# A hybrid decoder step on one core: the new tokens' state products moved from TensorE to VectorE, with the states transposed

## The chip, the cores and the metric

The kernel runs on one core of a Trainium2 chip. A core has five engines that each work through their own instructions in order and wait for one another by semaphores: PE (TensorE, matrix products; PEld is its weight load), DVE (VectorE), ACT (ScalarE), POOL (GpSimd) and SP (SyncE, which here only issues transfers). 16 DMA engines move data between the chip's memory (HBM) and the core's own memory. The metric is the device time of one execution in microseconds. All arithmetic is fp32. A large product is three passes over parts of its operands (a high part `hi` and a rest `lo` each: hi x hi, lo x hi, hi x lo).

## The reference

One layer of a decoder works on 512 prompt tokens and on 8 new tokens (a batch of 8 sequences, one token each): a feed-forward block, a token mixer, a second feed-forward block, each between norms. The mixer has two branches with 4 heads of 128 x 128 each. Every new token carries, for each branch and head, a state S of 128 (key dimension d) x 128 (value dimension e), 8 x 4 x 2 = 64 states in all. With one token per sequence the reference comes down to this for each state:

```
retention:   S' = gamma * S + k v^T                      o = q S'
DeltaNet:    S1 = exp(g) * S ;  u = beta * (v - k S1)
             S' = S1 + k u^T                             o = q S'
```

gamma is a constant of the head, exp(g) and beta belong to the token and head. o (per head normalized over e, then gated) goes on through the branch products `br`; S' is an output. The prompt tokens go through chunked forms of the same recurrences, which hold most of the mixer's small products.

## The kernel before

Features lie on partitions, tokens along the free dimension: 520 columns, 512 prompt and 8 new tokens, in two halves of 260. A product of weights with all tokens goes k-step by k-step, each step 2 halves x 3 passes of 128x260 (`passes`, L404 to L410). After each step the program calls `tick` (L223): this advances `now` by one, lets the weight prefetch go on, and resumes every spawned task (a Python generator) whose due time has come. A task that yields n is resumed n ticks later. So the order of instructions on each engine is fixed when the program is written: a task's instructions stand between two steps of the running product. `LATER` (L46) shifts single yields of single tasks by hand.

Weights come in raw tiles of 512 KB over SP (`load_to`, L270 to L289; two buffers), ACT makes the high part (L350), DVE the rest (L351); the splits run `AHEAD` = 2 products in front. Working tiles of 2 KB per partition come from one pool of 68 slots (`slot`, L247).

In the mixer (`mixer`, L1023) the projections follow `proj_order`: gates; then per head k, q, v of DeltaNet with their convolution; then per head RQ, RK, RV of retention; then RG and GZ (output gates), 4 each; then GR with the retention branch products and GG with the DeltaNet branch products. Each is 8 ticks. When a head's operands are there, its prompt part is spawned (`ret_head`, `gdn_head`); those tasks send small products to PE between the steps, and DVE, ACT and POOL work on their results. `gdn_head` needs the inverse of triangular matrices (`inverse`, L1484), whose substitution runs on POOL.

The new tokens' part has two tasks.

- `decode_gdn` (L1703) starts after the last DeltaNet projection: convolution and norms for 8 tokens, then `state_products` (L1654): states are loaded over SP, head by head, and for every token and head PE takes S as the stationary operand and the columns k and q as the moving one (L1665). From the two columns of results DVE makes u and o; o uses the identity q S' = q S1 + (q.k) u, with q.k from a column sum on PE (L1600). Then the norm, and `dec_done`.
- `decode_ret` (L1670) starts after the last RV and does the same with q alone.

After that each task runs `state_update` (L1629): u (or v) is transposed to rows, written to a scratch in HBM, read back as a broadcast to all partitions (L1635), the state is loaded a second time (L1651), ACT multiplies it with the decay (L1699 or L1757), DVE adds the outer product with d on partitions (L1643: broadcast row times the column k), and POOL issues the transfer out (L1646). A step of this is 18 ticks, eight steps for each branch.

The branch products wait at the end of each output gate stage (`while out not in done: self.tick()`) until `finish_decode` has put the new tokens' 8 columns into their operands.

Of the kernel before, what the change touches and what calls it, by code (L numbers as in the profile page):

```python
# [7 lines left out]
F32 = mybir.dt.float32  # L8
# [39 lines left out]
    ("decode_gdn", 0): {1: 8, 2: 2, 10: 3},  # L48
# [122 lines left out]
class Kernel:  # L171
# [851 lines left out]
    def mixer(self, xs, r, plus_next, x_from):  # L1023
# [26 lines left out]
        self.rdec = c.tile([P, 3, H, DEC], F32, name="rdec")  # L1050
        self.go, self.ro = [None] * H, [None] * H
# [5 lines left out]
        self.dec_done = set()  # L1057
        tiles, gate, lead = {}, {}, []

        def project(kind, h):  # L1060
# [16 lines left out]
            elif kind == RV:  # L1077
# [4 lines left out]
                if h == H - 1:  # L1082
                    self.spawn(self.decode_ret())
# [534 lines left out]
    def broadcast_rows(self, cols, name):  # L1618

        nc = self.nc  # L1620
        pt = self.bank("tr32")
        self.tr(pt[0:32, 0:P], cols)
        rows = self.slot(name, (32, P))
        nc.vector.tensor_copy(rows, pt[0:32, 0:P])
        d = self.dram.tile([32 * P], F32, name=self.name(name))
        nc.sync.dma_start(out=d.rearrange("(r e) -> r e", e=P), in_=rows)
        return d

    def state_update(self, rows, k, src, decay, out):  # L1629

        nc = self.nc
        for i in range(8):
            h, b0 = i // 2, 4 * (i % 2)
            rb = self.slot("rb", (P, 4, P))
            nc.sync.dma_start(  # L1635
                out=rb.rearrange("p b e -> p (b e)"), in_=rows[i * 512 : (i + 1) * 512].unsqueeze(0).to_broadcast([P, 512])
            )
            s = self.load_state(src, i)
            yield 14
            decay(s, h, b0)  # L1640
            yield 4
            for b in range(4):
                nc.vector.scalar_tensor_tensor(  # L1643
                    out=s[:, b, :], in0=rb[:, b, :], scalar=k[:, h, b0 + b : b0 + b + 1], in1=s[:, b, :], op0=ALU.mult, op1=ALU.add
                )
            nc.gpsimd.dma_start(out=out[:, h, b0 : b0 + 4, :], in_=s)  # L1646

    def load_state(self, src, i):
        h, b0 = i // 2, 4 * (i % 2)
        s = self.slot("sd", (P, 4, P))  # L1650
        self.nc.sync.dma_start(out=s, in_=src[:, h, b0 : b0 + 4, :])  # L1651
        return s

    def state_products(self, src, rhs, n):  # L1654

        nc = self.nc
        acc = self.cpool.tile([P, 32 * n], F32, name=self.name("sp"))
        load = lambda h: [self.load_state(src, i) for i in (2 * h, 2 * h + 1)]
        nxt = load(0)
        yield 12  # L1660
        for h in range(H):
            s, nxt = nxt, load(h + 1) if h < H - 1 else None
            ps = self.bank("sp")
            for b in range(DEC):
                nc.tensor.matmul(ps[:, b * n : (b + 1) * n], s[b // 4][:, b % 4, :], rhs(h, b), start=True, stop=True)  # L1665
            nc.vector.tensor_copy(acc[:, h * DEC * n : (h + 1) * DEC * n], ps[:, 0 : DEC * n])
            yield 14
        self.prod = acc

    def decode_ret(self):  # L1670
        nc, c = self.nc, self.cpool
        q, k, v = (self.rdec[:, i] for i in range(3))
        ks = c.tile([P, H, DEC], F32, name="rks")
        nc.vector.tensor_scalar(ks, k, DK_SCALE, None, ALU.mult)
        qk = self.const("rqk", [P, 32])
        nc.vector.tensor_tensor(qk, q, ks, ALU.mult)
        yield from self.state_products(self.a["sret"], lambda h, b: q[:, h, b : b + 1], 1)
        acc = self.prod
        t = c.tile([P, H, DEC], F32, name="rdo")
        nc.vector.tensor_tensor(t, v, self.column_sums(qk, 32), ALU.mult)  # L1680
        for h in range(H):
            nc.vector.scalar_tensor_tensor(
                out=t[:, h, :], in0=acc[:, h * 8 : h * 8 + 8], scalar=1.0 - 2.0 ** (-5.0 - h), in1=t[:, h, :], op0=ALU.mult, op1=ALU.add
            )
# [10 lines left out]
        rows = self.broadcast_rows(v.rearrange("p h b -> p (h b)"), "vrow")  # L1695
        yield 6

        def decay(s, h, b0):
            nc.scalar.mul(s, s, 1.0 - 2.0 ** (-5.0 - h))  # L1699

        yield from self.state_update(rows, ks, self.a["sret"], decay, self.a["srets"])

    def decode_gdn(self):  # L1703
# [20 lines left out]
        kq = c.tile([P, H, DEC, 2], F32, name="gkq")  # L1724
        rs4 = rs.rearrange("p (t h b) -> p t h b", t=2, b=DEC)
        kn = c.tile([P, H, DEC], F32, name="gkn")
        tt(kn, k, rs4[:, 1], ALU.mult)
        nc.vector.tensor_copy(kq[:, :, :, 0], kn)
        nc.vector.scalar_tensor_tensor(out=kq[:, :, :, 1], in0=q, scalar=DK_SCALE, in1=rs4[:, 0], op0=ALU.mult, op1=ALU.mult)
        qk = self.const("gqk", [P, H, DEC])  # L1730
        tt(qk, kn, kq[:, :, :, 1], ALU.mult)
        yield from self.state_products(self.a["sgdn"], lambda h, b: kq[:, h, b, :], 2)
        pm2 = self.prod.rearrange("p (h b t) -> p h b t", b=DEC, t=2)
        pqk = self.column_sums(qk, 32)
        eg, beta = self.dgb[:, 0], self.dgb[:, 1]
# [142 lines left out]
```

## Time and profile before

| | |
|---|---|
| runs shown | 1217.87, 1218.39 (median), 1218.42 us |
| profiled execution | span 1218.5 us; 0.1 us above the median, nothing is shown around it |
| PE / PEld busy | 1189.1 us (98%) / 1176.9 us (97%) |
| DVE / ACT / POOL busy | 899.6 us (74%) / 573.7 us (47%) / 277.1 us (23%) |
| transfers | 170.87 MB, mean 140 GB/s |
| mean granted clock of PE | 0.990 |

The page of a profile has the busy time of each engine, 40 slices of the span, the transfer queues, the chain of work that ended last (followed back from the last instruction), and the costliest groups of instructions. A row such as `L1665 PE MATMUL sp<-gkq,sd` is line 1665 of the kernel, the engine, the operation, and output<-inputs by the program's names. A row of a timeline begins with its start and its length in us. A row of windows begins with a stretch of time in us from the span's start.

### The profile page before, as it was taken

To read this page: it belongs to the slowest core of one execution; us is meant where nothing else is said; L and a number is where in the kernel's file an instruction comes from. 1 tells how busy PE (TensorE), PEld (TensorE's weight loads), DVE (VectorE), ACT (ScalarE), POOL (GpSimd) and SP (SyncE) were. 2 spreads that over 40 slices of the span, in tenths; PEclk is the share of its full clock that TensorE was granted. 3 is DMA by queue.
4 is the path that set the end of the run, shared out by engine and by line. 5 is a ranking of instruction groups with operands and counts; after the bars stand their busy time and mean duration, and the time that the engine had idled before them with its cause. 6 is when DMAs were issued, how large, how long until landed. Compare 5 with 4: busy or idle time off the path is not lost.

```text
span 1218.5 us, 25498 instructions
## 1 busy us (share of the span) xinstructions
PE 1189.1 (98%) x9937; PEld 1176.9 (97%) x9937; DVE 899.6 (74%) x1933; ACT 573.7 (47%) x1195; POOL 277.1 (23%) x502
## 2 busy tenths in 40 slices
PE   8999999999999999999999999999999999999995
PEld 7999999999999999999999999998999999999994
DVE  8988888776548787877666667546888888867554
ACT  6655666553335564313234334334565666653330
POOL 4211111000005148745541112203311111000003
PEclk8999999999999999999999999999999999999998
DMA  6787777133352533332444564342587777332352
GB/s 191 210 203 178 192 176 185 45 100 96 96 171 60 176 105 107 117 97 89 116 133 144 175 195 172 114 157 85 152 229 190 188 183 192 85 92 81 96 168 70
DMA packets 79689, 170.87 MB, mean 140 GB/s; under 512 B 17104, under 2 KB 20016, under 8 KB 79568
## 3 DMA queue, kind: packets, MB, share of 16 engines
q1 hardware_dynamic: 67280, 144.95, 37.4%
q0 software_dynamic: 12288, 24.29, 11.7%
q8 instruction: 78, 1.28, 0.4%
q14 instruction: 43, 0.35, 0.1%
HBM read 157.37 MB, written 11.83 MB: 139 GB/s over the span
## 4 chain that ended last, share of the span: by engine, by line
PE 88%; DVE 6%; ACT 2%; issue 1%; DMA 1%; POOL 1%; SPq 0%; DVEq 0%; ACTq 0%; POOLq 0%
PE sv L408 10%; PE sv L409 10%; PE sv L410 10%; PE p L408 7%; PE p L410 7%; PE p L409 7%; PE dn L408 7%; PE dn L409 7%; PE dn L410 7%; DVE wlo L351 2%; PE br L408 1%; PE br L409 1%; PE br L410 1%; PE g L409 1%; PE g L410 1%
## 5 line engine op out<-in xcount | busy, mean ns | idle before, releaser
L408 PE MATMUL p<-xhl,whi 128*128 128x260 f32 x784 | 231.0, 295 | 0.0
L409 PE MATMUL p<-xhl,whi 128*128 128x260 f32 x784 | 222.0, 283 | 1.4 <-DVE xhl L506 1.4
L410 PE MATMUL p<-xhl,wlo 128*128 128x260 f32 x784 | 221.3, 282 | 1.7 <-DVE wlo L351 1.7
L351 DVE TENSOR_TENSOR wlo<-raw,whi 128x1024 fp32r<-128x1024 f32 (+2 forms) x121 | 142.3, 1182 | 37.7 <-ACT whi L350 35.9
L408 PE MATMUL sv<-th,w 128*128 128x260 f32 x592 | 167.2, 282 | 0.5 <-ACT q L833 0.5
L409 PE MATMUL sv<-tl,w 128*128 128x260 f32 x592 | 167.1, 282 | 0.0
L410 PE MATMUL sv<-th,w 128*128 128x260 f32 x592 | 167.0, 282 | 0.0
L409 PEld LDWEIGHTS p<-xhl,whi 128*128 128x128 f32 x784 | 148.4, 189 | 2.0 <-DVE xhl L506 1.8
L410 PEld LDWEIGHTS p<-xhl,wlo 128*128 128x128 f32 x784 | 147.9, 189 | 2.1 <-DVE wlo L351 2.1
L408 PEld LDWEIGHTS p<-xhl,whi 128*128 128x128 f32 x784 | 148.1, 189 | 0.7
L350 ACT CAST whi<-raw 128x1024 fp32r<-128x1024 f32 (+2 forms) x121 | 116.4, 971 | 31.3 <-DMA raw<-dn_in 16.9
L369 DVE TENSOR_TENSOR w<-s,w 128x512 fp32r<-128x512 f32 x148 | 101.5, 688 | 37.9 <-ACT w L368 36.5
L307 POOL DMA_DIRECT2D s<-gu_in x74 | 65.1, 973 | 282.4 <-DMA s<-gu_in 143.8
L410 PE MATMUL dn<-hh,wlo 128*128 128x260 f32 x448 | 126.6, 283 | 1.2 <-DVE wlo L351 1.2
L408 PE MATMUL dn<-hh,whi 128*128 128x260 f32 x448 | 127.0, 283 | 0.0
L409 PE MATMUL dn<-hl,whi 128*128 128x260 f32 x448 | 126.7, 283 | 0.0
L409 PE MATMUL sv<-xhl,w 128*128 128x260 f32 x444 | 125.5, 283 | 0.0
L408 PE MATMUL sv<-xhl,w 128*128 128x260 f32 x444 | 125.4, 282 | 0.0
L410 PE MATMUL sv<-xhl,w 128*128 128x260 f32 x444 | 125.0, 281 | 0.0
L408 PEld LDWEIGHTS sv<-th,w 128*128 128x128 f32 x592 | 111.4, 188 | 0.9 <-ACT q L833 0.7
L410 PEld LDWEIGHTS sv<-th,w 128*128 128x128 f32 x592 | 111.6, 188 | 0.0
L409 PEld LDWEIGHTS sv<-tl,w 128*128 128x128 f32 x592 | 111.2, 188 | 0.0
(408 smaller groups left out, 3230.4 us busy)
## 6 DMA issues: line engine op xcount, KB each, us to landing
raw<-gu_in SPq DMA_DIRECT2D x50, 512.0 KB, 5.0
raw<-win_in SPq DMA_DIRECT2D x49, 512.0 KB, 3.6
s<-gu_in SPq DMA_DIRECT2D x74, 256.0 KB, 5.7
s<-gu_in POOLq DMA_DIRECT2D x74, 256.0 KB, 5.4
raw<-dn_in SPq DMA_DIRECT2D x32, 448.0 KB, 3.4
a<-gu_in SPq DMA_DIRECT2D x37, 256.0 KB, 5.9
x<-x SPq DMA_DIRECT2D x32, 260.0 KB, 5.1
raw<-dn_in SPq DMA_DIRECT2D x16, 512.0 KB, 3.7
```

The costliest lines, as they stand in the source:

```text
L307: self.nc.gpsimd.dma_start(out=out, in_=term, accum_op=ALU.add)
L350: self.nc.scalar.copy(hi[:, ks], t[:, ks])
L351: self.nc.vector.tensor_tensor(lo[:, ks], t[:, ks], hi[:, ks].bitcast(F32), ALU.subtract)
L369: nc.vector.tensor_tensor(w[:, 1], t[i], w[:, 0].bitcast(F32), ALU.subtract)
L408: mm(ps, hi[:, k, :], xh, start=first, stop=False, skip_group_check=more)
L409: mm(ps, hi[:, k, :], xl, start=False, stop=False, skip_group_check=more)
L410: mm(ps, lo[:, k, :], xh, start=False, stop=last, skip_group_check=more)
```

## The change

The states are laid out with the value dimension e on partitions (the host's transposition, done for inputs and outputs, is not part of the time). Then k S and q S are sums along the free dimension.

- `state_products`, `state_update`, `load_state` and `broadcast_rows` go, and with them L1665, both q.k column sums and the second load of each state.
- `row_scratch` transposes k and q columns on PE, copies them on DVE and writes them to a scratch in HBM over SP: once for DeltaNet (64 rows), once per head for retention (16 rows).
- `state_tile` loads four states of a head (256 KB) and the two broadcast tiles of rows of the same size.
- `state_dot` is a multiplication over 128x512 and a reduction over the last 128, both on DVE. `state_add` is the outer product's addition: four DVE instructions with the row k and the column v or u, and then the transfer out over POOL.
- Retention runs one task per head, spawned at its RV; a task waits until the one before is done. Each head has two halves of four tokens: load, 9 ticks, decay on ACT, 2 ticks, addition, 1 tick, dot with q (L1643's work and the output are now in the same pass).
- DeltaNet runs eight steps: load, 12 ticks, decay on ACT, 3 ticks, dot with k and u, 1 tick, addition, 1 tick, dot with q.
- `LATER` loses the entry 10 of `decode_gdn`.

The core of the diff:

```diff
-    ("decode_gdn", 0): {1: 8, 2: 2, 10: 3},
+    ("decode_gdn", 0): {1: 8, 2: 2},
...
-                if h == H - 1:
-                    self.spawn(self.decode_ret())
+                self.spawn(self.decode_ret(h))
...
+    def row_scratch(self, cols, n, name):
+        nc = self.nc
+        rows = self.slot(name, (n, P))
+        pt = self.bank("tr64")
+        self.tr(pt[0:n, 0:P], cols)
+        nc.vector.tensor_copy(rows, pt[0:n, 0:P])
+        d = self.dram.tile([n * P], F32, name=self.name(name))
+        nc.sync.dma_start(out=d.rearrange("(r e) -> r e", e=P), in_=rows)
+        return d
+    def state_tile(self, src, h, b0, rows):
+        nc = self.nc
+        s = self.slot("sd", (P, 4, P))
+        nc.sync.dma_start(out=s, in_=src[:, h, b0 : b0 + 4, :])
+        out = [s]
+        for r0 in rows[1:]:
+            t = self.slot("rb", (P, 4, P))
+            nc.sync.dma_start(
+                out=t.rearrange("p b e -> p (b e)"), in_=rows[0][r0 * P : (r0 + 4) * P].unsqueeze(0).to_broadcast([P, 4 * P])
             )
+            out.append(t)
+        return out
+    def state_dot(self, out, s, rows, to):
+        nc = self.nc
+        nc.vector.tensor_tensor(to, s, rows, ALU.mult)
+        nc.vector.tensor_reduce(out=out, in_=to, axis=AX.X, op=ALU.add)
+    def state_add(self, s, krow, col, out):
+        for b in range(4):
+            self.nc.vector.scalar_tensor_tensor(
+                out=s[:, b, :], in0=krow[:, b, :], scalar=col[:, b : b + 1], in1=s[:, b, :], op0=ALU.mult, op1=ALU.add
+            )
+        self.nc.gpsimd.dma_start(out=out, in_=s)
...
+        while len(self.ret_rows) < h:
+            yield 0
+        yield 2
+        both = self.small("rqk", [P, 2, DEC])
+        nc.vector.tensor_copy(both[:, 0], self.rdec[:, 0, h, :])
+        nc.vector.tensor_scalar(both[:, 1], self.rdec[:, 1, h, :], DK_SCALE, None, ALU.mult)
+        rows = self.row_scratch(both.rearrange("p t b -> p (t b)"), 2 * DEC, "rrow")
+        yield 6
+        v = self.rdec[:, 2, h, :]
+        for b0 in (0, 4):
+            s, qb, kb = self.state_tile(self.a["sret"], h, b0, (rows, b0, DEC + b0))
+            yield 9
+            nc.scalar.mul(s, s, 1.0 - 2.0 ** (-5.0 - h))
+            yield 2
+            self.state_add(s, kb, v[:, b0 : b0 + 4], self.a["srets"][:, h, b0 : b0 + 4, :])
+            yield 1
+            self.state_dot(self.rdo[:, h, b0 : b0 + 4], s, qb, qb)
+        self.ret_rows.append(h)
...
+        tt(kq[:, 0], k, rs4[:, 1], ALU.mult)
+        nc.vector.scalar_tensor_tensor(out=kq[:, 1], in0=q, scalar=DK_SCALE, in1=rs4[:, 0], op0=ALU.mult, op1=ALU.mult)
+        rows = self.row_scratch(kq.rearrange("p t h b -> p (t h b)"), 64, "grow")
+        yield 6
...
+        for i in range(8):
+            h, b0 = i // 2, 4 * (i % 2)
+            bs = slice(b0, b0 + 4)
+            s, kb, qb = self.state_tile(self.a["sgdn"], h, b0, (rows, h * DEC + b0, 32 + h * DEC + b0))
+            yield 12
+            for b in range(4):
+                nc.scalar.activation(s[:, b, :], s[:, b, :], AF.Copy, scale=eg[:, h, b0 + b : b0 + b + 1])
+            yield 3
+            self.state_dot(u[:, h, bs], s, kb, self.slot("sk", (P, 4, P)))
+            tt(u[:, h, bs], v[:, h, bs], u[:, h, bs], ALU.subtract)
+            tt(u[:, h, bs], u[:, h, bs], beta[:, h, bs], ALU.mult)
+            yield 1
+            self.state_add(s, kb, u[:, h, bs], self.a["sgdns"][:, h, bs, :])
+            yield 1
+            self.state_dot(o[:, h, bs], s, qb, qb)
```

More of the change, by code (lines that the diff above doesn't have):

```diff
@@ L1646, in state_update @@
[L1646 to L1654, printed above, removed]
-        nc = self.nc
[L1657 to L1668, printed above, removed]
@@ L1694, in decode_ret @@
         self.dec_done.add(RG)
[L1695 to L1701, printed above, removed]
     def decode_gdn(self):
@@ L1751, in decode_gdn @@
         self.dec_done.add(GZ)
-        rows = self.broadcast_rows(u.rearrange("p h b -> p (h b)"), "urow")
-        yield 6
-        def decay(s, h, b0):
-            for b in range(4):
-                nc.scalar.activation(s[:, b, :], s[:, b, :], AF.Copy, scale=eg[:, h, b0 + b : b0 + b + 1])
-        yield from self.state_update(rows, kn, self.a["sgdn"], decay, self.a["sgdns"])
     def finish_decode(self, kind):
```

67 lines of the change are left out of this document (12 added, 55 removed).

## The prediction

> **What bounds the kernel now.** I read the page first (busy shares, then the chain that ended last), then the windows around the new tokens' work, then single lines.
>
> ```profile
> span 1218.5 us, 25498 instructions
> PE 1189.1 (98%) x9937; PEld 1176.9 (97%) x9937; DVE 899.6 (74%) x1933; ACT 573.7 (47%) x1195; POOL 277.1 (23%) x502
> PE 88%; DVE 6%; ACT 2%; issue 1%; DMA 1%; POOL 1%; SPq 0%; DVEq 0%; ACTq 0%; POOLq 0%
> ```
>
> TensorE carries 88% of the chain, so an instruction taken from PE shortens the program by its own length, as long as nothing else then arrives late. VectorE is only 74% busy overall, but that is a mean over stages. The stage of this change runs from about 488 to 772 us. The windows give, after each stretch and its length, the busy time of PE, PEld, DVE, ACT and POOL:
>
> ```profile
> 430.00:490.00 60.00, 60.00 (x508) 60.00 (x507) 48.83 (x131) 32.02 (x87) 38.93 (x84) 1.00 0.34 100
> 505.00:530.00 25.00, 25.00 (x229) 24.55 (x228) 21.27 (x62) 6.75 (x10) 14.74 (x38) 1.00 0.34 111
> 530.00:567.00 37.00, 36.67 (x339) 36.07 (x337) 25.10 (x78) 9.08 (x20) 17.35 (x49) 1.00 0.32 95
> 567.00:629.00 62.00, 62.00 (x555) 60.69 (x555) 42.15 (x124) 21.24 (x43) 28.60 (x80) 1.00 0.38 116
> 629.00:663.00 34.00, 34.00 (x294) 33.35 (x294) 22.33 (x72) 13.58 (x34) 11.25 (x30) 1.00 0.46 141
> 663.00:772.00 109.00, 109.00 (x930) 108.46 (x929) 72.40 (x179) 41.87 (x84) 15.96 (x25) 1.00 0.54 172
> ```
>
> At 81% DVE (48.83 of 60) PE still runs without a gap. Where DVE needs more, it becomes the chain: in 396 to 413 us, the convolution stage, the chain is
>
> ```profile
> by line: DVE cv L1276 36.0%; POOL rs L465 13.3%; ACT cv L1274 12.9%; issue 10.5%; PE rb L477 9.3%; DVE cin L1268 7.6%; DVE wlo L351 7.2%; DVE rows L1167 3.9%; DVE rb L557 2.5%; PE p L410 2.3%; PE p L408 0.7%; PE p L409 0.7%; DVEq L1184 0.1%
> ```
>
> So the question is how much room DVE has in the stage that the change fills.
>
> **What is removed.** The state products (L1665), 64 products in two passes each, eight groups of 16 passes on PE:
>
> ```profile
> L1665 PE MATMUL sp<-gkq,sd x64: 165/251/251, 515.5 to 567.0; 128*128 128x2 f32 x64
> L1665 PE MATMUL sp<-rdec,sd x64: 166/250/271, 582.6 to 632.9; 128*128 128x1 f32 x64
> 515.63 1.68 PE sp L1665 x16
> L1600 PE MATMUL cs<-gqk,ones x2: 190/232/273, 586.5 to 586.5; 128*128 128x32 f32 x2
> 511.66 0.44 PE tr L1162 x4
> ```
>
> A group holds the chain for 1.68 us: 8 x 1.68 = 13.4 us. The two column sums of the q.k products (232 ns a pass, overlapped) and two row transposes go, five row transposes come (0.44 / 4 = 0.11 each): about nothing. PE's side is -13.4 us. Groups lie at 515, then three before 567, three before 629, one at 631.
>
> **What is added on DVE.** Twenty-four dots (8 for retention, 16 for DeltaNet), each a multiplication and a reduction over 128x512. The trace has the multiplication's form but no reduction:
>
> ```profile
> 514.69 0.67 DVE L1434 TENSOR_TENSOR gkd<-gkd,cols 128x512 f32<-128x512 f32 x1
> 515.29 0.68 DVE L1437 TENSOR_TENSOR cv<-tr,cols 128x512 f32<-128x512 f32 x1
> L1353 DVE BATCH_NORM_STATS2 bs<-po 128x6 f32<-128x128 f32 x16 | 4.4, 274 | 6.2 <-ACT ro L1350 6.2
> L1643 DVE SCALAR_TENSOR_TENSOR sd<-rb,gkn,sd x32: 332/343/348, 630.2 to 738.5; 128x128 f32<-128x128 f32 x32
> 630.21 1.12 DVE L1643 SCALAR_TENSOR_TENSOR sd<-rb,gkn,sd 128x128 f32<-128x128 f32 x4
> 770.57 1.14 DVE L1643 SCALAR_TENSOR_TENSOR sd<-rb,rks,sd 128x128 f32<-128x128 f32 x4
> 504.44 0.18 DVE L1728 COPY gkq<-gkn 128x32 f32<-128x32 f32 x1
> ```
>
> Back to back a 512-wide pass takes 0.60 (514.69 to 515.29). For the reduction the nearest rows bound it by four statistics passes over 128 elements (4 x 0.274 = 1.10) above, and below by half a two-input pass (0.30), since it has one input instead of two. I take 0.65, the pass that also streams 512 elements once: a dot is 1.25 us, ends 0.9 and 1.7. Together 30 us. The page "VectorE: DVE Perf Modes" of the Trainium skill (perf-mode tier table) lists the reduction at one element a cycle only, the rate it lists for a two-input pass in this type; no run here shows that yet.
>
> The 16 state additions (1.13 us each, 18 us) are not new but move: L1643 ran at 630 to 772, behind everything; now each stands in front of its dot. ACT's decays move with them, on an engine 25 to 40% busy in these windows.
>
> **Where it lands.** A tick is one step of the running product. In the old order the DeltaNet products start at the tick 53 before the last value projection (RV, head 3), and the retention output is due 78 ticks after it:
>
> ```profile
> L1651 SPq DMA_DIRECT2D sd<-sgdn_in x16: 327/424/433, 502.6 to 719.6; - x16
> L1080 POOL COPY rdec<-rv x4: 189/981/1120, 487.2 to 566.3; 128x8 f32<-128x8 f32 x4
> 652.43 0.19 DVE L1615 COPY rdr<-cb 128x32 f32<-128x32 f32 x1 [1.63 <-PE cb L1614]
> ```
>
> That is 1.2 us a tick before 566 and 1.1 after. Retention: 2 + 6 + 2 x (9 + 2 + 1) = 32 ticks a head, one head after the other, from 488 to 57 ticks behind 566, about 629. A head is two dots, two additions and three small operations: 2.5 + 2.26 + 0.5 = 5.3 us; four in 141 us are 0.15 us per us. Its output then is ready at tick 67, twelve ticks earlier than before, so the wait for it ahead of the branch products goes. DeltaNet: eight steps of 17 ticks, from about 528 to 665: 2 x 1.25 + 1.13 + 2 x 0.18 = 4.0 us a step, 0.235 us per us. Its output comes at tick 99, needed at about 176: no wait. With what the old order had there taken out (copies, the u chain, three additions after 629):
>
> - 505 to 530: DVE 21.3 + 3.8 - 0.2 = 24.9; PE 25 - 1.7 = 23.3
> - 530 to 567: DVE 25.1 + 0.385 x 37 - 0.5 = 38.8; PE 37 - 5.0 = 32.0
> - 567 to 629: DVE 42.2 + 23.9 - 2 = 64.1; PE 62 - 5.0 = 57.0
> - 629 to 663: DVE 22.3 + 8.0 - 4.4 = 25.9; PE 34 - 1.7 = 32.3
>
> In the first three, 124 us long, DVE needs 127.8: it sets the pace, +3.8 in place of PE's -11.7. The fourth is PE's, -1.7. DVE can end the third late and catch up in the fourth (6.4 us of room) by as much as it may lag without stopping PE. The old trace shows such a lag:
>
> ```profile
> 498.44 0.29 PEld L1614 LDWEIGHTS cb<-cst,gdm 64*128 64x128 f32 x2
> 499.72 0.47 PEld L1539 LDWEIGHTS pV<-pack,AT 32*32 32x32 f32 x16
> 503.32 0.21 DVE L1615 COPY gdr<-cb 128x64 f32<-128x64 f32 x1
> 504.53 0.18 DVE L1729 SCALAR_TENSOR_TENSOR gkq<-dcv,gdr 128x32 f32<-128x32 f32 x1
> ```
>
> The norm's columns leave PE at 498.7 and DVE takes them at 503.3: 4.6 us behind. That lends -4.5.
>
> After 663 DVE, ACT and the queues lose the old updates, but PE is full there (108.5 of 109): nothing to gain.
>
> **New waits.** row_scratch multiplies on DVE and transposes on PE in one tick, with no step between. PE stands there until DVE has come through its backlog, and all products behind it in PE's order wait. For DeltaNet the rows above price it: PE reaches the place at about 499.7, kq is done at 504.7, so up to 5.0 us. Afterwards DVE has about 2 us of work in hand and PE's next results come 5 us later, so about 3 us of DVE time is lost. Retention has four such places; their lag is not in the trace. Between 0 and 5 each, I take 1.4, as two ticks (2.3 us) have passed since the previous dot. Together 3 + 5.6 = 8.6, bounds 0 and 24. No row prices them better.
>
> The queues:
>
> ```profile
> L1635 SPq DMA_DIRECT2D rb<-urow x8: 327/420/432, 609.8 to 719.1; - x8
> DMA to landing us min/median/max: 3.9/5.0/6.7
> SPq L287 <- DVE wlo L351: 96.4, 16, 10.5
> L1646 POOL DMA_DIRECT2D sgdns_out<-sd x8: 539/542/626, 631.6 to 739.2; - x8
> L1360 POOL TENSOR_TENSOR rsr<-var,mhalf 128x4 f32<-128x4 f32 x4 | 4.2, 1045 | 3.9 <-DVE gs L1480 2.6 <-DVE rks L1674 1.3
> ```
>
> SP: each step now issues a state and two broadcasts, 9 or 12 ticks (10 or 13 us) ahead of use, where it was 14; landing takes 5 to 7 us, but SP stands in front of weight loads, up to 10.5 us.
>
> I price this at nothing: the total of such transfers stays 48 of 256 KB (16 states instead of 32, 32 broadcasts instead of 16), and the landing hides under the ticks. POOL's output transfers stand behind DVE's additions, ahead of the powers and the inverse's steps; POOL is 47% busy there (28.60 of 62), so nothing too.
>
> **Sum.** +3.8 - 1.7 - 4.5 + 8.6 = +6.2 us on the profiled 1218.5, which lies 0.1 above the median 1218.39 of the runs, so 1224.6; I say **1225**. The dot's ends move it by about 20 x 0.35 = 7 down and 20 x 0.45 = 9 up, as some 20 dots lie in the three windows.
>
> **Rivals.**
> - *DVE takes it all in its gaps* (faster): PE keeps its -13.4 less three short stops of 1.4, 1209 (1203 to 1216). It decides once DVE's need in the three windows, 127.8, falls to PE's 112.3 plus the lag it can owe, 4.5: 11 us less, a dot of 0.7, or the cheap dot (-7) with a debt of 8.5. For it: 81% ran without a gap, and the weight splits (L351) are made two products ahead, so a debt there may last longer than the 4.6 us seen. Against: three windows over 100%, and the stop at DeltaNet's rows.
> - *Even*: the lag and a cheap reduction eat just the overload, 1218 (1216 to 1221).
> - *Late transfers*: an SP that stands up to 10.5 us in front of a weight load lets states and rows land after 10 us; ACT and DVE stand in order behind them:
>
> ```profile
> ACT sd L1699 <- DMA sd<-sret_in: 3.7, 2, 2.1
> ```
>
>   Two of the eight old decays waited, 1.85 each, under a lead of 14 ticks. If all eight do under 9, 15 more: 1240. Against: six did not.
> - *The clock*: after a stop PE runs slower for a while:
>
> ```profile
> 411.00:413.60 2.60, 1.20 (x10) 1.15 (x10) 2.44 (x10) 0.20 (x1) 0.17 (x1) 1.00 0.01 2
> 422.00:424.00 2.00, 2.00 (x13) 1.98 (x13) 1.93 (x4) 2.00 (x11) 0.00 (x0) 0.63 1.02 384
> 424.00:426.00 2.00, 2.00 (x11) 2.00 (x11) 1.97 (x5) 1.53 (x9) 1.74 (x2) 0.51 0.54 204
> ```
>
>   PE stood 1.4 us, and nine us later the clock was 0.63 and 0.51 for 2 us each, 0.74 + 0.98 = 1.7 us lost. Three such dips after the new stops give 1230. The Trainium skill's page "TensorE: Matmul & The Clock Gate" (Part 1) has the gate halve the clock after an idle window of about 3.4 us; by that only the stop of 5 us would count. The trace has a dip after a shorter stop.
>
> **Chances.** Forecast (1221 to 1232) 0.40, all in gaps 0.28, even 0.20, late transfers 0.08, clock 0.04. A measurement here tells about 0.2% (2.4 us) from no change. So faster 0.28, the same 0.20, slower 0.52. The range reaches into both signs: 1206 to 1242.
>
> **What would show it.** Right: 505 to 629 with DVE above 95% busy, PE waiting for DVE at the row transposes (5 us at DeltaNet's), the chain there on DVE lines, and 13.4 us of L1665 gone. The reduction's row settles its price. Wrong: DVE under 90% with PE's waits still there (then the stops are the cost), waits of ACT or DVE for states and rows (the transfers), or PE full through the stage and a time near 1207.

## The result, and the profile after

| | before | after |
|---|---|---|
| median of the runs | 1218.41 us | 1265.22 us (1263.48 to 1265.87) |
| ratio | | 1.0383, 95% interval 1.0371 to 1.0396 |
| profiled execution, span | 1218.5 us | 1264.1 us |
| mean granted clock of PE | 0.990 | 0.972 |

The change makes the kernel 46.8 us slower. The profile's first part and the chain of the kernel after:

```profile
span 1264.1 us, 25318 instructions
PE 1194.7 (95%) x9808; PEld 1180.7 (93%) x9808; DVE 934.6 (74%) x1985; ACT 573.8 (45%) x1195; POOL 282.4 (22%) x502
PE 69%; DVE 16%; issue 5%; ACT 5%; DMA 2%; POOL 2%; SPq 1%; DVEq 0%; ACTq 0%; POOLq 0%
```

PE has 129 instructions less and yet 5.6 us more of busy time, and its share of the chain falls from 88% to 69%. The stretches that the prediction used, in the kernel after (busy PE, PEld, DVE, ACT, POOL, then PE's granted clock):

```profile
505.00:530.00 25.00, 22.48 (x183) 21.71 (x183) 19.07 (x63) 7.76 (x14) 10.43 (x28) 0.87 0.42 131
530.00:567.00 37.00, 29.80 (x242) 29.44 (x243) 31.27 (x85) 8.70 (x20) 19.19 (x42) 0.90 0.51 148
567.00:629.00 62.00, 48.61 (x376) 47.18 (x376) 46.12 (x134) 17.21 (x37) 26.69 (x66) 0.86 0.42 137
629.00:663.00 34.00, 25.60 (x206) 24.56 (x206) 27.05 (x69) 11.78 (x28) 14.71 (x43) 0.80 0.45 145
```

No engine is full: in the first three stretches DVE is busy 96.5 of 124 us (78%), PE 100.9 (81%), and PE's clock lies at 0.86 to 0.90. That is the prediction's own sign for "the stops are the cost". What PE waits for from 470 to 800 us, first in the kernel before, then in the kernel after (total us, times, longest):

```profile
PE pV L1560 <- DVE pack L1552: 0.3, 1, 0.3
```

```profile
PE tr L1163 <- DVE rqk L1665: 20.8, 4, 7.7
PE pS L1458 <- DVE AT L1455: 4.6, 2, 4.0
PE cs L1601 <- DVE rdo L1648: 4.2, 1, 4.2
PE pV L1540 <- DVE pack L1530: 3.6, 2, 2.7
PE tr L1163 <- DVE gkq L1716: 2.5, 1, 2.5
```

The five row transposes (L1163) hold PE for 23.3 us, the head chains and the column sums for most of another 18. The longest single stop, on PE and on DVE:

```profile
573.12 0.38 PE L1454 MATMUL pu<-cv,TT 128*128 128x128 f32 x2
581.16 0.38 PE L1163 MATMUL tr<-cst,rqk 128*16 128x128 f32 x1 [7.66 <-DVE rqk L1665]
```

```profile
568.57 2.02 DVE L1653 SCALAR_TENSOR_TENSOR sd<-rb,rdec,sd 128x128 f32<-128x128 f32 x4
571.48 0.43 DVE L1293 TENSOR_TENSOR rp<-p,cos 128x260 f32<-128x260 f32 x1 [0.89 <-DMA sgdns_out<-sd]
...
574.85 1.22 DVE L351 TENSOR_TENSOR wlo<-raw,whi 128x1024 fp32r<-128x1024 f32 x1
575.99 0.68 DVE L1647 TENSOR_TENSOR rb<-sd,rb 128x512 f32<-128x512 f32 x1
576.71 0.69 DVE L1648 TENSOR_REDUCE rdo<-rb 128x4 f32<-128x512 f32 x1
...
580.87 0.16 DVE L1664 COPY rqk<-rdec 128x8 f32<-128x8 f32 x1
580.94 0.17 DVE L1665 TENSOR_SCALAR rqk<-rdec 128x8 f32<-128x8 f32 x1
```

PE is through with its work at 573.5 and asks for `rqk`, two instructions of 0.16 us. They stand in DVE's order behind the rotary products, a weight split, a dot and the pieces of two head chains: 9.4 us without a gap. Ahead of that the addition took 2.02 us instead of the 1.1 of others, and a slot that an output transfer still held cost 0.89. PE pays for the whole line, not for the instruction that it needs. Right behind the stop, in stretches of 2 us, come PE's slow ones (the clock had fallen while PE still stood, first row):

```profile
576.00:578.00 2.00, 0.00 (x0) 0.00 (x0) 1.90 (x6) 0.00 (x0) 1.69 (x6) 0.61 0.35 66
582.00:584.00 2.00, 2.00 (x11) 2.00 (x11) 0.00 (x0) 0.00 (x0) 0.00 (x0) 0.50 0.02 4
588.00:590.00 2.00, 2.00 (x11) 2.00 (x10) 0.00 (x0) 0.15 (x1) 0.00 (x0) 0.50 0.04 8
590.00:592.00 2.00, 2.00 (x18) 2.00 (x18) 1.40 (x7) 0.44 (x1) 0.00 (x0) 0.97 0.02 4
```

For 9 us after the restart PE gets half its clock (11 passes in 2 us instead of 18), and DVE, which had work for 9 us without a gap, has almost none until 590. This stop thus is paid twice, and the engine that caused it then starves.

**An account.** For each profile I divide 470 to 800 us into slices of 10 us and add up what PE stood ("stood") and, as time lost to the clock, (1 - granted clock) x busy PE of each slice ("clock"). Both, less the 0.3 of the kernel before, less the products that are gone (13.4, or 6.7 where one part of the change is made) should be the difference of the spans from 1218.5. It is, within 3.4 us, for every kernel run. The last five columns are of the one profiled execution, the first two of all runs; the profiled one can lie off the median (idle dots 4.5 us above it, halves together 5.2 below). A run's time is 1.7 to 1.85 us longer than its span (after: 1265.87 and 1264.1), so the profiled execution before, of which only the span is on record, lies by this some 1.8 us above its median, not 0.1, and the last column is lower than the medians would give by about as much:

| kernel | median us | ratio (95%) | stood | clock | products | sum | span - 1218.5 |
|---|---|---|---|---|---|---|---|
| after | 1265.22 | 1.0371 to 1.0396 | 41.6 | 21.1 | -13.4 | +49.0 | +45.6 |
| before, five stops | 1241.65 | 1.0178 to 1.0209 | 14.4 | 5.5 | 0 | +19.6 | +21.0 |
| before, 24 idle dots | 1223.41 | 1.0022 to 1.0062 | 4.0 | 3.1 | 0 | +6.8 | +7.6 |
| rows early | 1240.48 | 1.0167 to 1.0197 | 25.9 | 9.3 | -13.4 | +21.5 | +20.5 |
| no dots | 1239.16 | 1.0161 to 1.0197 | 27.2 | 6.8 | -13.4 | +20.3 | +18.9 |
| rows early, no dots | 1219.40 | 0.9996 to 1.0014 | 10.7 | 4.5 | -13.4 | +1.5 | -1.6 |
| rows early, halves together | 1246.73 | 1.0199 to 1.0239 | 29.9 | 7.0 | -13.4 | +23.2 | +21.2 |
| rows early, no dots, longer lead | 1221.48 | 1.0015 to 1.0035 | 10.3 | 5.9 | -13.4 | +2.5 | +3.0 |
| retention alone | 1243.10 | 1.0187 to 1.0215 | 22.4 | 7.1 | -6.7 | +22.5 | +22.6 |
| DeltaNet alone | 1231.88 | 1.0102 to 1.0130 | 12.6 | 5.8 | -6.7 | +11.4 | +11.7 |
| retention alone, rows early | 1227.03 | 1.0061 to 1.0095 | 6.8 | 4.3 | -6.7 | +4.1 | +4.1 |
| rows early, DeltaNet 76 ticks later | 1229.99 | 1.0076 to 1.0103 | 16.4 | 6.7 | -13.4 | +9.4 | +10.2 |
| the same, halves together | 1228.84 | 1.0065 to 1.0093 | 14.9 | 9.5 | -13.4 | +10.7 | +10.2 |
| DeltaNet alone, late | 1220.16 | 1.0006 to 1.0024 | 5.9 | 1.6 | -6.7 | +0.5 | -0.7 |
| DeltaNet alone, latest | 1219.87 | 1.0003 to 1.0021 | 6.4 | 0.0 | -6.7 | -0.6 | -1.6 |
| whole change, best placed | 1221.83 | 1.0013 to 1.0031 | 10.7 | 1.6 | -13.4 | -1.4 | -1.0 |

The products were put in as forecast. Taken the other way round, the difference of the spans less standing and clock leaves -12.6 to -16.8 in the nine versions of the whole change, -6.4 to -7.9 in the five with one part, and +0.8 and +1.4 where nothing was removed. So the gain is there in every version; what differs is how long PE stands, mostly for DVE, and how much clock it loses.

### The profile page after: what moved, and what is told of

Its sections match the earlier page's. It is cut to its first block, busy times and chain, and to the rows that moved or that the text cites. A ratio compares the mean times of both kernels' runs of the same rounds, so it can differ in the third digit from the quotient of the medians.

```text
span 1264.1 us, 25318 instructions
## 1 busy us (share of the span) xinstructions
PE 1194.7 (95%) x9808; PEld 1180.7 (93%) x9808; DVE 934.6 (74%) x1985; ACT 573.8 (45%) x1195; POOL 282.4 (22%) x502
## 4 chain that ended last, share of the span: by engine, by line
PE 69%; DVE 16%; issue 5%; ACT 5%; DMA 2%; POOL 2%; SPq 1%; DVEq 0%; ACTq 0%; POOLq 0%
PE sv L408 10%; PE sv L409 10%; PE sv L410 10%; PE dn L410 7%; PE dn L408 7%; PE dn L409 7%; DVE wlo L351 4%; PE p L408 3%; PE p L410 3%; PE p L409 3%; DVE cv L1277 1%; ACT whi L350 1%; PE br L408 1%; PE br L410 1%; PE br L409 1%
## 5 line engine op out<-in xcount | busy, mean ns | idle before, releaser
L408 PE MATMUL p<-xhl,whi 128*128 128x260 f32 x784 | 237.1, 302 | 0.0
L409 PE MATMUL p<-xhl,whi 128*128 128x260 f32 x784 | 227.7, 290 | 1.4 <-DVE xhl L506 1.4
L410 PE MATMUL p<-xhl,wlo 128*128 128x260 f32 x784 | 226.8, 289 | 1.8 <-DVE wlo L351 1.8
L409 PEld LDWEIGHTS p<-xhl,whi 128*128 128x128 f32 x784 | 154.3, 197 | 2.0 <-DVE xhl L506 1.8
L410 PEld LDWEIGHTS p<-xhl,wlo 128*128 128x128 f32 x784 | 153.7, 196 | 2.2 <-DVE wlo L351 2.2
L408 PEld LDWEIGHTS p<-xhl,whi 128*128 128x128 f32 x784 | 154.1, 197 | 0.7
L369 DVE TENSOR_TENSOR w<-s,w 128x512 fp32r<-128x512 f32 x148 | 101.6, 689 | 38.2 <-ACT w L368 36.6
L350 ACT CAST whi<-raw 128x1024 fp32r<-128x1024 f32 (+2 forms) x121 | 116.3, 970 | 26.1 <-DMA raw<-dn_in 15.9
```

What stands on the lines that cost most here:

```text
L350: self.nc.scalar.copy(hi[:, ks], t[:, ks])
L369: nc.vector.tensor_tensor(w[:, 1], t[i], w[:, 0].bitcast(F32), ALU.subtract)
L408: mm(ps, hi[:, k, :], xh, start=first, stop=False, skip_group_check=more)
L409: mm(ps, hi[:, k, :], xl, start=False, stop=False, skip_group_check=more)
L410: mm(ps, lo[:, k, :], xh, start=False, stop=last, skip_group_check=more)
```

## The experiments

### What stops and dots cost by themselves

First theory: the loss is made by the row transposes, where PE stands for DVE's whole line of work. Rival: DVE has too much to do with 24 dots more. Each was put alone into the kernel before.

Five row transposes right behind DVE's columns, no dots (`stop` transposes on PE and copies on DVE):

```diff
+    def ret_stop(self, h):
+        ...
+        yield 2 + 8 * h
+        both = self.small("rqk", [P, 2, DEC])
+        ...
+        self.stop(both.rearrange("p t b -> p (t b)"), 16)
...
         tt(qk, kn, kq[:, :, :, 1], ALU.mult)
+        self.stop(kq.rearrange("p h b t -> p (h b t)"), 64)
```

> The kernel before with five row transposes added at the places of the change (each right behind the DVE operations that make its input, at the ticks of the changed kernel), whose rows are not used; no dots, nothing removed. Theory A: five stops of 2 to 5 us and a dip of the clock after most, 15 to 30 us, 1233 to 1248. Theory B: five short instructions and small waits on a DVE at 70%, 3 to 8 us, 1221 to 1226.

Measured: 1241.65 us, +23.2, in the range of theory A. PE's waits there from 470 to 800 us:

```profile
PE tr L1163 <- DVE rqk L1682: 11.7, 4, 4.0
PE tr L1163 <- DVE gkq L1744: 2.8, 1, 2.8
```

14.5 us of waiting at these five places and nowhere else, and 5.5 of clock. DVE's lag behind PE (1.3 to 4.0 us at retention's places) was there in the kernel before, where nothing asked for it.

The 24 dots on zeros, at the change's ticks, nothing waits for them:

```diff
+    def dot(self):
+        ...
+        self.nc.vector.tensor_tensor(t, self.da, self.da, ALU.mult)
+        self.nc.vector.tensor_reduce(out=o, in_=t, axis=AX.X, op=ALU.add)
+    def ret_dots(self, h):
+        yield 2 + 8 * h + 18
+        self.dot()
+        yield 12
+        self.dot()
+    ...
```

> The kernel before with 24 dots on a tile of zeros added on DVE at the ticks of the change (two every 17 ticks, and two a retention head); PE's products stay, no new transposes, nothing waits for their results. Theory A: DVE takes most of 29 us in its gaps, PE loses 0 to 8 us, 1218 to 1226. Theory B: the overload alone costs most of the dots, 15 to 30 us, 1233 to 1248.

Measured: 1223.41 us, +4.9, in the range of theory A. PE's waits are short, in the head chains (470 to 800 us; the longest group):

```profile
PE pV L1561 <- DVE pack L1553: 2.6, 3, 1.8
```

The dots alone cost a fifth of what the stops cost. But +23.2 + 4.9 - 13.4 is +14.7, and +46.8 was measured: some 32 us come from what the two do together and from what else moved.

### One of them taken out of the change

The rows' columns made at the task's start, 8 ticks ahead of their transposes; DeltaNet's likewise:

```diff
-        while len(self.ret_rows) < h:
-            yield 0
-        yield 2
-        both = self.small("rqk", [P, 2, DEC])
+        both = self.const("rqk", [P, 2, DEC])
         ...
+        yield 8
+        while len(self.ret_rows) < h:
+            yield 0
         rows = self.row_scratch(both.rearrange("p t b -> p (t b)"), 2 * DEC, "rrow")
...
+        yield 8
         rows = self.row_scratch(kq.rearrange("p t h b -> p (t h b)"), 64, "grow")
```

> The changed kernel with DVE's small operations for the row transposes set 8 ticks ahead of the transposes (retention: as each head's task starts, before it waits for the head in front; DeltaNet: 8 ticks between kq and its transpose). Theory A (PE stops at the row transposes for a DVE that is behind, and its clock falls after each stop): the 23.3 us of stops at these transposes go, and most of the about 21 us that the lower clock costs, so 1220 to 1235. Theory B (DVE is simply given too much in this stage, and PE has to stand for it somewhere): PE stands in the DeltaNet heads' chains instead, 1250 or more.

Measured: 1240.48 us, 24.7 less than the change, between the two ranges. PE's waits (470 to 800 us):

```profile
PE pV L1561 <- DVE pack L1553: 6.6, 2, 5.8
PE pu L1454 <- DVE cv L1449: 5.4, 1, 5.4
PE pV L1540 <- DVE pack L1530: 3.7, 1, 3.7
PE ks L1448 <- DVE S L1464: 3.6, 2, 3.4
```

No row transpose stops PE for its columns any more, and half of the loss is gone. The other half shows at new places: PE now reaches the prompt chains' steps before DVE has done them. (This also moves the steps behind the transposes, those of DeltaNet and of retention's first head by 8 and 6 ticks, so it is not the stops alone that change.)

The change with each dot replaced by a 128x4 multiplication:

```diff
-        nc.vector.tensor_tensor(to, s, rows, ALU.mult)
-        nc.vector.tensor_reduce(out=out, in_=to, axis=AX.X, op=ALU.add)
+        nc.vector.tensor_tensor(out, s[:, :, 0], rows[:, :, 0], ALU.mult)
```

> The changed kernel with all 24 dots left out: a multiplication of 128x4 elements stands in for each, so u and the new tokens' outputs and states are not those of the reference; transposes, transfers, additions and places are as in the changed kernel. 24 x about 1.2 = 29 us of DVE less. Theory A: DVE still lags some us where it is asked for rows in the same tick; the stops and dips shrink by about half, 1225 to 1240. Theory B: DVE is under its limit again and PE keeps the 13.4 us of the products, 1205 to 1215.

Measured: 1239.16 us, 26.1 less than the change, in the range of theory A; but the stops did not shrink by half, as it has it. PE's waits (470 to 800 us), and DVE's for transfers (490 to 660 us):

```profile
PE tr L1163 <- DVE rqk L1664: 21.6, 4, 9.8
PE tr L1163 <- DVE gkq L1715: 2.6, 1, 2.6
```

```profile
DVE sd L1652 <- DMA rb<-rrow: 2.7, 1, 2.7
DVE rp L1293 <- DMA sgdns_out<-sd: 1.9, 1, 1.9
```

The waits at the transposes are as long as with the dots (24.2 against 23.3 us); PE's other waits shrink from 18 to 3 us, and the clock loss by two thirds (21.1 to 6.8). So the dots are not what makes retention's four stops longer than the 11.7 of the run with stops alone. The 32 us left open above come in two parts: 10.9 are there without any dot (1239.16 is 20.7 above before, and stops alone less the products give +9.8), and 21.2 are what the dots cost on top of their 4.9 alone (26.1). The longest, 9.8 us, lies behind an addition that stood for its row and a rotary product that stood for a slot which an output transfer still held: 4.6 us of DVE standing, ahead of the rows in its order.

Both together, rows early and no dots:

> The kernel of the early rows (no stops at the transposes) and the 24 dots left out, a multiplication of 128x4 elements in the place of each, so that new tokens' outputs and states are not those of the reference. What is left of the change: PE without its products, the additions, decays and transfers at their new places. Theory A (the rest of the loss under early rows is dots and additions together over what DVE has): without the dots DVE stays under its limit and PE keeps most of the 13.4 us, 1204 to 1212. Theory C (the moved additions, decays, outputs and their transfers stand in front of other work on DVE, ACT, POOL and SP): the 11 us by which the run without dots exceeded the sum of the parts stay, 1214 to 1222.

Measured: 1219.40 us, ratio 0.9996 to 1.0014: as before, and not 13.4 us faster; the range of theory C. Against rows early (1240.48) the dots cost 21.1 us here. What is left is 10.7 us of standing and 4.5 of clock. ACT's and DVE's waits for transfers (490 to 660 us) and SP's order show the source of the longest stop:

```profile
ACT sd L1671 <- DMA sd<-sret_in: 10.9, 3, 5.4
DVE sd L1652 <- DMA rb<-rrow: 4.1, 1, 4.1
```

```profile
530.75 5.60 SPq L1520 DMA_DIRECT2D s<-pack  x8
537.67 1.77 SPq L1523 DMA_DIRECT2D pack<-s  x4
539.49 0.45 SPq L1634 DMA_DIRECT2D sd<-sret_in  x1
539.98 0.91 SPq L1638 DMA_DIRECT2D rb<-rrow  x2
```

The eight small transfers of an inverse hold SP for 5.6 us, and the state tile of retention, due 9 ticks later, is issued only behind them. ACT stood 4.3 us for that tile, DVE 4.1 for its row; behind DVE's addition came two rotary products, a split and the transpose that PE needs, and PE stood 5.6 us.

### Late transfers

Two attempts to ask earlier. Both halves of a retention head loaded at once, so the second is 12 ticks earlier:

```diff
+        two = [self.state_tile(self.a["sret"], h, b0, (rows, b0, DEC + b0)) for b0 in (0, 4)]
         for b0 in (0, 4):
-            s, qb, kb = self.state_tile(self.a["sret"], h, b0, (rows, b0, DEC + b0))
+            s, qb, kb = two[b0 // 4]
```

> Early rows, DeltaNet where the change has it, both halves of a retention head loaded at once (the second half 12 ticks earlier). Theory A: no change of more than 3 us from early rows, 1238 to 1243. Theory C: the waits of ACT for states (7.7 us in two places under early rows) and what hangs on them go, 1228 to 1235.

Measured: 1246.73 us, 6 more than with rows early alone, and in neither range. The profiled execution is the fastest of the four, 1241.50, level with that of rows early (1240.81), so no trace shows where the 6 us lie. It does show that ACT's waits for retention states (7.7 us with rows early) are gone and that this gained nothing. ACT now stands ahead of the decay for something else (480 to 700 us):

```profile
ACT kd L1315 <- DMA sretp_out<-st: 12.0, 1, 12.0
```

This is a slot of the pool that an output of the prompt part still held, and PE's wait at L1530 is 6.6 us instead of 3.7. That the tiles loaded ahead made the slots scarce is likely, but not shown.

Then, without dots, the first half asked for 14 ticks ahead (rows transposed ahead of the head's turn):

```diff
         yield 8
+        rows = self.row_scratch(both.rearrange("p t b -> p (t b)"), 2 * DEC, "rrow")
+        yield 6
         while len(self.ret_rows) < h:
             yield 0
-        rows = self.row_scratch(both.rearrange("p t b -> p (t b)"), 2 * DEC, "rrow")
-        yield 6
         ...
-            yield 9
+            yield 9 if b0 else 14
```

> As the version with early rows and without dots (each dot replaced by a 128x4 multiplication, so the products are left out), and beside it retention's rows are transposed before the head waits for its turn, and each head's first state tile is asked for 14 ticks ahead of its use instead of 9. Theory that late transfers carry the 13 us which that version lacks to a full gain of 13.4: PE's 5.6 us stop for pack is gone, no ACT wait for a retention state over 1 us, 1206 to 1212. Rival, that the moved additions themselves do it: 1217 to 1222, with DVE's waits for states gone and PE's waits there.

Measured: 1221.48 us, no gain against 1219.40, in the range of the rival. ACT's largest wait for a retention state fell from 5.4 to 2.1 us and PE's wait at L1530 is 0.3 instead of 5.6, but now DVE stands elsewhere (490 to 650 us):

```profile
DVE pack L1541 <- DMA rrow<-rrow: 5.0, 1, 5.0
```

and PE 3.5 us behind it. The late tile was a cause of its own stop; that late transfers are all of the missing 13 us is not shown. With the transfer put earlier, DVE waits for a slot that the write of the rows still holds.

### The two parts alone

Retention's part as in the change, DeltaNet's as before, and the other way round (each is the diff's half; the other half's functions and state layout stay as in the kernel before).

> The change's retention part alone (four row transposes, 8 dots, 8 state additions moved, 32 of the 64 products gone); DeltaNet's part is as in the kernel before. Theory that the stops at retention's transposes carry most of the loss: they stay, 12 to 18 us of waiting PE <- rqk, each with slow slices behind it, less 6.7 us of products: 1230 to 1242. Rival, that the loss comes from both parts meeting on DVE (24 dots and 16 additions at once): with a third of the dots the stops are short, under 8 us in all, and the time is 1216 to 1226.

Measured: 1243.10 us, +24.7, above the range of the theory of the stops. PE's largest group of waits (470 to 780 us, as for DeltaNet alone below):

```profile
PE tr L1163 <- DVE rqk L1717: 18.5, 4, 7.1
```

> The change's DeltaNet part alone (one row transpose, 16 dots, 8 additions moved, 32 products gone); retention's part is as in the kernel before. Theory that retention's stops carry the loss: one stop of 2.5 us and some 2 us of slow clock, less 6.7: 1214 to 1222. Rival, that DVE's load carries it (two thirds of the dots lie here): 1228 or more, with PE waiting for DVE in the head chains. If losses of the two parts simply add, this run's and the retention run's differences from before sum to 47; if they come from the parts meeting, to 30 or less.

Measured: 1231.88 us, +13.5, in the rival's range: beside one stop of 4.1 us at the transpose PE stands some 8 us for DVE in the head chains and column sums, and 5.8 us go to the clock. PE's longest waits:

```profile
PE tr L1164 <- DVE gkq L1768: 4.1, 1, 4.1
PE pV L1541 <- DVE pack L1531: 2.2, 1, 2.2
```

24.7 and 13.5 are 38.2 of 46.8: most of the loss lies in the parts themselves, 8.6 in their meeting. Retention's part loses by stops, as the theory has it. DeltaNet's loses by more than its one stop, as its rival has it; that DVE's load is the cause there is argued from the lines at which PE waits, since no run took this stop alone out of it. In retention alone the stops at its transposes are nearly all that PE stands for. To see whether they are also the cause, its rows were made early, as above, in that part alone:

> Retention's part alone, with its rows' columns made 8 ticks ahead of the transposes; everything else as in that part alone (1243.1). Theory that the four stops at its transposes (18.5 us, and the slow slices behind them) are its loss: no PE <- rqk wait over 0.5 us and 1216 to 1224. Rival, that the eight dots and additions ahead of the products, or late states, stop PE elsewhere instead: 1228 or more, with PE waiting for DVE's pack, AT or rdo.

Measured: 1227.03 us, 16.1 less than 1243.10. The waits at the transposes are gone; left are these (470 to 780 us), and 4.3 us of clock:

```profile
PE pV L1561 <- POOL pack L1515: 1.9, 1, 1.9
PE ks L1448 <- DVE S L1464: 1.9, 1, 1.9
PE cs L1601 <- DVE rdo L1648: 1.8, 1, 1.8
```

So two thirds of retention's loss are those four stops and what hangs on them; the result lies between the two expectations, since short stops elsewhere still use up the 6.7 us of products.

### Another place for the dots

With rows early, DeltaNet's steps 76 ticks later (15 ticks each, the next tile loaded a step ahead), where DVE has room:

```diff
-        yield 6
+        yield 82
         ...
+        nxt = tile_of(0)
         for i in range(8):
             ...
-            s, kb, qb = self.state_tile(self.a["sgdn"], h, b0, (rows, ...))
-            yield 12
+            s, kb, qb = nxt
+            if i < 7:
+                nxt = tile_of(i + 1)
+            yield 10
```

> Early rows, and DeltaNet's eight steps begin 76 ticks later, behind retention's in place of beside them, 15 ticks each with the next step's state and rows loaded one step ahead; its output is due at tick 167 of the 176 it has. The same work for DVE, spread over 505 to 760 us. Theory A (too much for DVE at one time): DVE stays under about 85% in each stretch and PE keeps nearly all of its gain, 1205 to 1213. Theory C (the places of additions and transfers themselves, in order on their queues): the waits move with them, 1218 to 1235.

Measured: 1229.99 us, 10.5 less than with rows early alone, in the range of theory C. The condition of theory A, DVE under 85% in each stretch, was not met: it is 94% busy in 505 to 530 us, 84% in 567 to 629. With both retention halves loaded at once beside it:

> As the run before it, and both halves of a retention head's states and rows are loaded at once, so the second half has 21 ticks in place of 9. Theory A: within 2 us of the run before it. Theory C (late transfers hold ACT and DVE): 3 to 8 us less than it.

Measured: 1228.84 us; the intervals of the two overlap, as theory A has it, though ACT's waits for retention states fall from 8.7 to 3.0 us (480 to 700 us). DeltaNet alone at that later place:

> DeltaNet's part alone, rows transposed 8 ticks after their columns are made, the eight steps 76 ticks later and each state tile loaded a step ahead; retention as before. The dots then lie in 620 to 760, where DVE was 66% busy. Theory that place and stops set the price and not the dot: no stop at the transpose, DVE under 90% there, 6.7 us of products gone less 1 to 3 us of short waits: 1212 to 1216, faster than before. Rival, that dots on DVE cost PE more than its products wherever they are put: 1219 to 1225.

Measured: 1220.16 us, ratio 1.0006 to 1.0024, the rival's range. PE's longest waits (470 to 780 us):

```profile
PE cs L1602 <- DVE rdo L1723: 3.0, 1, 3.0
PE br L409 <- DVE ol L1819: 1.6, 1, 1.6
```

and, to get out of the way of these, 28 ticks later still, in steps of 13:

> As DeltaNet alone and late, its steps another 28 ticks later and 13 ticks long instead of 15, so that no dot lies ahead of retention's column sums (3.0 us of PE's wait there, 1.6 at the branch). Theory that the place of the dots sets their price: those two waits shrink to under 1 us and the time is 1212 to 1217. Rival, that it saves nothing wherever it is put: 1219 to 1224, with PE waiting for DVE at other lines.

Measured: 1219.87 us, ratio 1.0003 to 1.0021. Those two waits are gone, as expected; the time is not, which was the rival's forecast: others of the same sum came (470 to 800 us).

```profile
PE br L408 <- ACT oh L1815: 2.1, 2, 1.2
PE pS L1459 <- DVE AT L1456: 1.8, 2, 1.1
PE cs L1609 <- DVE gosq L1799: 1.3, 1, 1.3
```

Last, the whole change with all of this (rows early and ahead of the head's turn, first retention tile 14 ticks ahead, DeltaNet 104 ticks later in steps of 13):

> The whole change with retention's rows early and transposed ahead of the head's turn, its first state tile asked for 14 ticks ahead, and DeltaNet's steps 104 ticks later than in the change, 13 ticks long and loaded a step ahead. Theory that retention's dots and DeltaNet's cost each other DVE's room only while they meet: the sum of the two parts placed well, 1214 to 1222. Rival, that retention's dots and moved additions stop PE's head chains by themselves: 1226 to 1232, as with DeltaNet 76 ticks later (1230.0).

Measured: 1221.83 us, ratio 1.0013 to 1.0031, at the upper end of the theory's range. All dots, all additions and all transfers of the change are in it: 43.4 of the 46.8 us were a matter of where they stood. No version was faster than the kernel before.

## Why the prediction was wrong

The direction was forecast (slower, at 0.52), the size was not: 1225 with a range up to 1242, and 1265 was measured. The sign came from the term of the stops (without its 8.6 the sum is -2.4), and the stops are the largest part of what the runs show, so it was not luck; the size of that term is what failed. By the steps of the prediction:

**Products, -13.4: right as an amount.** The account closes with this term in all sixteen rows. The sum did not grant it in 505 to 629 us, as DVE was to set the pace there.

**The price of a dot, 1.25 us: right.** The rows of the change:

```profile
L1647 DVE TENSOR_TENSOR rb<-sd,rb x16: 651/686/693, 508.1 to 709.0; 128x512 f32<-128x512 f32 x16
L1648 DVE TENSOR_REDUCE rdo<-rb x8: 685/686/686, 508.8 to 677.1; 128x4 f32<-128x512 f32 x8
```

Back to back a dot takes 1.32 us (from 575.99 above to the next instruction at 577.31). The reduction takes as long as the two-input pass; the table of the Trainium skill's page "VectorE: DVE Perf Modes" (perf-mode tier table), one element a cycle for both, agrees.

**DVE sets the pace in 505 to 629, +3.8 in place of -11.7: not seen in the change.** This is a price of 15.5 us for a full DVE. Over those 124 us DVE is 78% busy in the change and 87% (107.3 us) with rows early; near full it is only there, and only in the first 25 us (95%). The dots had a price all the same, and not a fixed one: 4.9 us alone, 21.1 with rows early, 26.1 in the change. It shows as waits of PE, mostly for single results of DVE, and as clock, not as a pace.

**"That lends -4.5": failed, and with the wrong sign.** The lag of 4.6 us that the old trace showed was taken as credit, up to which DVE may be late at no cost. It is no credit where PE asks for the newest thing in DVE's line: there PE pays the lag that DVE has at that moment, at this very place 2.5 us in the change, 2.8 with stops alone and 4.1 in DeltaNet alone.

**"New waits", 8.6: the step that failed most.** DeltaNet's stop was put at 3 us and measured 2.5. Retention's four were put at 1.4 each "as two ticks (2.3 us) have passed since the previous dot", with 5 as the upper end; they measured 3.3, 5.7, 7.7 and 4.1, together 20.8. The dot ahead is 1.3 us of a line of 9.4. With stops alone, without any dot, they were 3.5, 2.9, 4.0 and 1.3, so the kernel before held most of this lag already, at these ticks. What else moved made it longer (21.6 in the run without dots); additions that stood for their rows and a slot still held are seen in front of the longest stop there, but no run divides this share. The waits in the prompt's head chains and column sums, 18 us in the change, were not in the sum at all.

**The clock: a rival at 0.04 that is a part of nearly every case.** Priced at 1.7 us a dip with three dips, it cost 21.1 us. In the five runs where PE stood for more than 20 us it comes to 0.23 to 0.51 of that time (7.0 of 29.9, 7.1 of 22.4, 21.1 of 41.6), in the others to anything from 0 to 0.78. So it belonged into the sum as a share of the stops, not beside it, but no single factor fits. The dip that the prediction read from the old trace is a weak sign for it: in the kernel after PE stands about as long at the same place (1.45 us in 408 to 412 us), and its clock stays at 1.00 up to 432 us.

**The queues, "priced at nothing": not at nothing, how much is open.** By the run with neither stops nor dots there are 15 us of standing and clock left, which just use up the gain; one of the stops was followed to SP's eight transfers ahead of a state tile. The rival "late transfers" named ACT's wait for states; the traces show it for the retention tiles (10.9 us in that run). How the 15 us divide between late transfers, slots still held and the moved additions stays open: asking earlier moved the waits and saved nothing.

The forecast treated PE's gain, DVE's load, the stops and the transfers as terms to be added. Stops alone and dots alone, less the products, give +14.7. Of the other 32 us, 10.9 come without any dot, from additions, decays and transfers at their new places, and 21.2 are what the dots cost more there than alone. The trace of the longest stop shows one way in which such things meet: PE waits for a long line on DVE, loses clock behind it, and DVE then has almost no work for 9 us.

## What to carry to other kernels

Where a step makes a value on one engine and uses it on the bottleneck engine in the same step, its price is the whole lag of the first engine at that place, and in most runs here some lost clock on top: read that lag from the trace before the change, and put some steps between, as here, where 8 ticks saved 16 us in one part and 25 in the whole (with the steps behind them moved by some ticks too). A busy share of 74% on the helper says nothing of that lag. And 13 us taken from the full engine for 32 us of new work (24 dots of 1.32) on an engine that feeds it were worth, at the best place found here, nothing: the short waits that this brings add up to the gain.

## What the runs showed of the hardware that was not expected

**Half clock after short stops.** In retention alone with rows early PE stood 1.9 us in the four us before 532, and then had 0.50 for about 7 us:

```profile
530.00:532.00 2.00, 0.73 (x7) 0.74 (x7) 1.93 (x6) 0.37 (x2) 1.76 (x5) 1.00 0.41 155
534.00:536.00 2.00, 2.00 (x10) 2.00 (x11) 0.17 (x1) 0.00 (x0) 0.00 (x0) 0.50 0.29 80
```

A stop of 1.25 us (at 618.4, in the run with stops alone) was followed by 0.70 and 0.50 in the next four us, while five stops of 0.7 to 1.3 us in DeltaNet alone, latest, had none; and in the run with idle dots the clock fell to 0.50 at 536 to 538 us though PE had stood for 0.01 us in the twelve us before. So the length of one stop does not decide it alone in these traces. The Trainium skill's page "TensorE: Matmul & The Clock Gate" (Part 1) gives an idle window of about 3.4 us as the condition; the stops named here were shorter, and the measurement decides. That the clock falls to one half agrees (0.50).

**The moment of the drop.** At the stop of 7.7 us, which began at 573.5, the clock was 1.00 up to 576 us, 0.61 in 576 to 578 and 0.50 behind that: it fell about three us after PE stopped, and came back nine us after the restart at 581.2.
